# An encoder block with expert retrieval on one core: matmul operands placed at multiples of 512 bytes, two kinds of transfers issued elsewhere and earlier

## The chip, the core and the metric

The kernel runs on one core of a Trainium2 chip. The metric is the device time of one execution, in microseconds; lower is better. The median of three runs of the kernel before is 1516.14 us (1514.39 to 1519.15).

A core has five engines with a queue each: TensorE (PE: matmuls, and PEld, the load of a matmul's stationary operand), VectorE (DVE), ScalarE (ACT), GpSimd (POOL) and SyncE (SP). DMAs are started from the queues of SP, ACT and POOL. Each queue works in order.

## What is computed

512 tokens of 1024 channels go through a mixer (pooling and a short convolution, gated) and then through an expert layer, which holds most of the work:

```python
x = x + m @ w_out[l]                                  # m: the gated mixer
h2 = rmsnorm(x, g_ffn[l])
x = x + peer_ffn(h2, w_q[l], sub_keys[l], expert_u[l], expert_v[l])

# peer_ffn, per token, 8 heads:
q = (hb @ w_q).reshape(PEER_TOKEN_BLOCK, PEER_HEADS, 2, PEER_HALF)
s = jnp.einsum('thpc,hpkc->thpk', q, sub_keys)        # 2 x 128 key scores
top_s, top_i = lax.top_k(s, PEER_TOPK)                # 16 best of each half
cand_s = top_s[:, :, 0, :, None] + top_s[:, :, 1, None, :]
fin_s, fin_pos = lax.top_k(cand_s, PEER_TOPK)         # 16 best pairs -> idx, gates
act = jax.nn.gelu(jnp.einsum('thkd,td->thk', expert_u[idx], hb))
out = jnp.einsum('thk,thkd->td', gates * act, expert_v[idx])
```

There are 16384 experts (128 x 128), and each token uses 8 x 16 of them.

## The kernel before

All matmuls of width 256 to 512 work on a high and a low part of each operand (`split` makes them, `mm3` issues the three products, lines 58 to 60). The order of all work is the order of the code: a manual schedule, with nothing reordered. The stages, with the time at which they run:

- **Mixer** (to about 290 us). Weights come as `raw` tiles through `w_plan`, are split into `wh` and `wl` (ACT copies, POOL or DVE subtracts), and are the stationary operands; the normed input `hH`, `hL` (or the branches' `pHL`, `yHL`) is the moving one, 512 columns wide. In the output projection the mixer's result `mH`, `mL` is stationary and the weights move. A weight tile is laid out as [partition, k, 256], and a matmul takes 128 of the 256.
- **Queries and keys** (290 to 510 us). `load_q` brings and splits the query weights, `queries` multiplies them with `h2H`, `h2L`, VectorE picks the top 16s. Between them `u_tick` already runs chunks of the expert layer.
- **Chunks of the up projection.** There are 128 chunks of 128 experts. For each, `u_load` (SP) brings `ur`, `u_high` and `u_low` split it into `uH`, `uL`, `u_mm` does 24 matmuls of 320 columns with `uH`, `uL` stationary, and `u_act` writes `a` (ACT, a Gelu) and, for the first 76 chunks, stores it to `Ad` in HBM from ACT's queue.
- **Building the gates** (about 510 to 780 us, 48 steps). Dense gates of 384 tokens are built by matmuls of one-hots: `one_hots` (DVE compares, ACT scales by `cgate`), 8 products of 128 x 128 on line 858, `to_stage` (ACT copies the result into `stage`). When a stage of 32 tokens is full, ACT stores it to `Gd` in two halves of 1 MB (line 766); 11 of the 12 stages go there. Each step also holds one chunk of the up projection (`u_load(i + 3)`, `u_high(i + 2)`, `u_low(i + 2)`), and two calls of `gather`: for the last 128 tokens, and for the up projection of 64 of the 384, rows of experts are gathered (POOL) and multiplied on VectorE (lines 719, 724), expert by expert. Near the end the dot products of those 64 tokens, `mdots`, go through a Gelu (ACT, line 835) and a product with `mgate` (DVE, line 836), and then through `mgates` (PE, line 824) into `cgate`.
- **Outputs** (about 780 to 1500 us, 128 steps). Step i loads `expert_v` (`v_load`, split into `vH`, `vL`), the gates of four chunks at a time (`g_load`, 704 KB) and the stored activations (`a_load`), forms `wH`, `wL` = gates x activations (`weigh`, `weigh_low`), and does 18 matmuls of 512 columns (line 904) with `wH`, `wL` stationary and `vH`, `vL` moving. From step 75 on, each step also holds one chunk of the up projection.

Where the tiles lie in a partition follows from the pools' order of allocation. In the built program of the kernel before, the starts of TensorE's operands stand this many bytes past a multiple of 512: `uH`, `uL` 352; `vH`, `vL`, `wH`, `wL` 96; `mH`, `mL` 160; `wh`, `wl` 480; `gwH`, `gwL` 416; `hH`, `h2H` and their low parts 256; `pHL`, `yHL` 416; the one-hots 96. So no stationary tile of 128 columns (512 bytes) starts at a multiple of 512, and each runs over one.

Of the kernel before, what the change touches and what calls it, by code (L numbers as in the profile page):

```python
# [16 lines left out]
P = 128  # L17
D = 1024
T = 512
# [28 lines left out]
def block_kernel(ctx: ExitStack, tc: tile.TileContext, io, out, dbg=None):  # L48
# [3 lines left out]
    def split(Hd, Ld, src, pool=False):  # L52

        nc.scalar.copy(Hd, src)  # L54
        (nc.gpsimd if pool else nc.vector).tensor_tensor(Ld, src, f(Hd), ALU.subtract)  # L55
# [13 lines left out]
    def rbank(lo=0, hi=8):  # L69
        ring[0] += 1  # L70
        return bank(lo + ring[0] % (hi - lo))

    keep = ctx.enter_context(tc.tile_pool(name="keep", bufs=1))
    work = ctx.enter_context(tc.tile_pool(name="work", bufs=2))

# [3 lines left out]

    for tag, w, n in (("u", T, 2), ("s", T, 2), ("p", T, 2), ("up", T + 2, 2), ("sg", T, 4)):  # L80
        fpool.tile([P, w], F32, tag=tag, name=tag, bufs=n)
    pHL = fpool.tile([P, 2, 4, T], F32R, tag="pHL", name="pHL")
    pH, pL = pHL[:, 0], pHL[:, 1]
# [5 lines left out]
    gb = fpool.tile([P, D], F32, tag="gb", name="gb")  # L89
    w0 = [wpool.tile([P, DC, 256], t, tag=n, name=n) for n, t in (("raw", F32), ("wh", F32R), ("wl", F32R))]  # L90

# [3 lines left out]
    def w0_load(e):  # L95
        nc.sync.dma_start(w0[0][:, :, e * P:(e + 1) * P], io["w_in"][0, :, :, e * P:(e + 1) * P])

# [11 lines left out]

    warm = keep.tile([P, 1], F32, name="warm")  # L110
    nc.vector.memset(warm, 1.0)
    nc.scalar.activation(warm, warm, AF.Sqrt)
    cold = fpool.tile([P, T], F32, tag="sg", name="cold", bufs=4)
    nc.vector.memset(cold, 0.0)
    for k in range(4):
        nc.tensor.matmul(bank(7), cold[:, :P], cold, start=True, stop=True)
    pscale = keep.tile([P, 4], F32, name="pscale")
    nc.gpsimd.dma_start(pscale, io["pool_scale"])
    cw = keep.tile([P, 12], F32, name="cw")
    nc.gpsimd.dma_start(cw, io["conv_w"])  # L120
# [3 lines left out]
    nc.gpsimd.iota(iota, pattern=[[1, P]], base=0, channel_multiplier=0, allow_small_or_imprecise_dtypes=True)  # L124
    rcnt = fpool.tile([P, 4, 16], F32, name="rcnt")
    for g, w in enumerate((2, 4, 8, 16)):
# [43 lines left out]
    raws_w, ws_q = {}, []  # L170

    def w_load(k):

        if k < len(w_plan):
            src, n, m, _, _ = w_plan[k]
            raws_w[k] = wpool.tile([P, n, m], F32, tag="raw", name="raw")
            nc.sync.dma_start(raws_w[k], src)
# [3 lines left out]
    def w_next():  # L181

        k = n_w[0]
        n_w[0] += 1
        if k < len(w_plan):
            _, n, m, pool, dst = w_plan[k]
            wh, wl = dst() if dst else [wpool.tile([P, n, m], F32R, tag=t, name=t) for t in ("wh", "wl")]
            split(wh, wl, raws_w.pop(k), pool=pool)
            w_load(k + 2)
            ws_q.append((wh, wl))  # L190
# [4 lines left out]
    def z_part(o, w, u, t0, t1):  # L195
        for k in range(DC):
            mm3(o[:, t0:t1], w[0][:, k, u * P:(u + 1) * P], w[1][:, k, u * P:(u + 1) * P], hH[:, k, t0:t1], hL[:, k, t0:t1],
                k == 0, k == DC - 1)

# [30 lines left out]
    def w0_split(e):  # L230
        es = slice(e * P, (e + 1) * P)
        nc.scalar.copy(w0[1][:, :, es], w0[0][:, :, es])
        for k in (slice(0, 4), slice(4, 8)):
            nc.gpsimd.tensor_tensor(w0[2][:, k, es], w0[0][:, k, es], f(w0[1][:, k, es]), ALU.subtract)

# [104 lines left out]
    def branch(w, aH, aL, u):  # L340
        o = rbank()
        for k in range(4):
            mm3(o, w[0][:, k, u * P:(u + 1) * P], w[1][:, k, u * P:(u + 1) * P], aH[:, k], aL[:, k], k == 0, k == 3)
        return o
# [26 lines left out]

    nc.scalar.activation(warm, warm, AF.Sqrt)
    hn = keep.tile([P, NT - KD, D], F32, name="hn")
# [93 lines left out]
    def load_q(h):  # L467
        raw = wpool.tile([P, DC, 256], F32, tag="raw", name="raw")
        wh = wpool.tile([P, DC, 256], F32R, tag="wh", name="wh")
        wl = wpool.tile([P, DC, 256], F32R, tag="wl", name="wl")  # L470
        nc.sync.dma_start(raw, io["w_q"][h])
        nc.scalar.copy(wh, raw)
        for k in (slice(0, 4), slice(4, 8)):
            nc.gpsimd.tensor_tensor(wl[:, k], raw[:, k], f(wh[:, k]), ALU.subtract)
        return wh, wl
# [20 lines left out]

    rank0 = qpool.tile([P, TOPK], F32, name="rank0")
    nc.vector.tensor_scalar(rank0, iota[:, :TOPK], 2.0, 1.0, op0=ALU.mult, op1=ALU.max)
# [27 lines left out]
    def queries(w, s):  # L526
        o = bank(2 + s)
        for k in range(DC):
            mm3(o, w[0][:, k, s * P:(s + 1) * P], w[1][:, k, s * P:(s + 1) * P], h2H[:, k], h2L[:, k], k == 0, k == DC - 1)
        q = qpool.tile([P, T], F32, tag="q", name="q", bufs=2)  # L530
        nc.scalar.copy(q, o)
        return q
# [93 lines left out]
    gate = qpool.tile([P, NT, H, TOPK], F32, tag="sc2", name="gate", bufs=1)  # L626
    zs = qpool.tile([P, NT, H], F32, tag="zs", name="zs", bufs=1)
    nc.vector.tensor_tensor(gate, fv, fv[:, :, :, 0:1].to_broadcast([P, NT, H, TOPK]), ALU.subtract)
# [124 lines left out]

    built, stages = {}, {}

    def to_stage(n):

        t1 = 4 * n % TG
        if t1 == 0:
            stages[0] = (lpool if (4 * n // TG) % 2 == (NG - 1) % 2 else spool).tile([P, NK, TG], F32, tag="stage", name="stage")  # L760
        stage = stages[0]
        nc.scalar.copy(stage[:, :, t1:t1 + 4], built.pop(n).rearrange("p (t i) -> p i t", t=4))
        if t1 + 4 == TG and 4 * n // TG < NG - 1:
            for q in range(2):
                ks = slice(q * 64, q * 64 + 64)
                nc.scalar.dma_start(Gd[4 * n // TG, :, ks], stage[:, ks])

# [16 lines left out]
    def a_load(i):  # L784
        if i < n_ahead:
            abs_[i] = bpool.tile([P, TU], F32, tag="ab", name="ab", bufs=3)
            nc.sync.dma_start(abs_[i], Ad[i])
# [41 lines left out]
    for n in range(0, TD // 4, 2):  # L829
        left = TD // 4 - n  # L830
        if TM and left == TM // 4 + 6:

            assert n_done[0] >= NM
            ms_ = mdots[:, TM:2 * TM]
            nc.scalar.activation(ms_, ms_, AF.Gelu)
            nc.vector.tensor_tensor(ms_, ms_, mgate, ALU.mult)
        i = nu[0]
        nu[0] += 1
        u_load(i + 3)
        u_high(i + 2)  # L840
        one_hots(n + 2)
        if n:
            to_stage(n - 2)
            to_stage(n - 1)
# [3 lines left out]
        if left == 4:  # L848
            g_load(0)
            a_load(0)  # L850
            a_load(1)
        if 24 <= left < 30:
# [104 lines left out]
    for i in range(NK - 1):  # L957
        v_load(i + 3)
        g_load(i + 2)
        g_rest(i + 2)  # L960
        a_load(i + 2)
        both = i + 1 >= n_ahead
# [26 lines left out]

    nc.scalar.activation(warm, warm, AF.Sqrt)  # L990
    last = range(NK - 3, NK)
# [71 lines left out]
```

## Time and profile before

| | |
|---|---|
| median of three runs | 1516.14 us |
| the profiled execution, its own time | 1516.17 us |
| its span, first to last instruction | 1514.4 us |
| PE busy | 1469.5 us, 97% |
| DVE busy | 1209.5 us, 80% |
| ACT, POOL busy | 682.2 us, 694.5 us |
| moved by DMA | 415.7 MB, 275 GB/s over the span |

The profile has one line per group of instructions, stretches of the span with the busy time of each engine, what each wait was for, and the start of each instruction. Matmuls are pipelined, so a busy PE says little: what one matmul costs is read from the distance between the starts of matmuls that follow each other without a wait. A wait counts if the engine that waits is the one that sets the pace of its stage.

### The profile page before, as it was taken

What the parts mean: (1) busy time and instruction counts of PE and PEld (TensorE: products, weight loads), DVE (VectorE), ACT (ScalarE), POOL (GpSimd) and SP (SyncE); (2) the same over time, 40 slices, a digit from 0 to 9 for tenths busy, and PEclk for the clock granted to TensorE, in tenths of its full rate; (3) what the DMA queues carried; (4) which work ended last, traced back from release to release, by engine and by line L of the source; (5) the groups of instructions that cost most, each with busy time, mean ns of one, the idle gap of its engine ahead of it and who ended that gap; (6) DMA issues with size and microseconds to landing.
All of it is one profiled execution on the core that took longest, in us unless ns stands there. A gap on an engine that the chain in (4) does not pass through costs nothing.

```text
span 1514.4 us, 22020 instructions
## 1 busy us (share of the span) xinstructions
PE 1469.5 (97%) x7953; PEld 1289.3 (85%) x7953; DVE 1209.5 (80%) x2238; ACT 682.2 (45%) x1196; POOL 694.5 (46%) x432
## 2 busy tenths in 40 slices
PE   8999999999997989999999999999999999999997
PEld 6788888878887989999897878888889999999996
DVE  5841433549999899999877888888899999999975
ACT  4323223433324678878763433333333343333434
POOL 3432322337774577766223333333255555556610
PEclk9999999999999999999999999999999999999999
DMA  5222223442213799999989999999999999999951
GB/s 188 84 98 84 84 97 113 128 162 111 111 55 126 277 373 385 401 386 395 361 309 373 351 363 372 359 350 374 363 380 388 378 387 387 390 383 380 394 210 70
DMA packets 163356, 415.71 MB, mean 275 GB/s; under 512 B 13744, under 2 KB 80304, under 8 KB 156848
## 3 DMA queue, kind: packets, MB, share of 16 engines
q1 hardware_dynamic: 102992, 210.99, 39.0%
q0 software_dynamic: 46144, 167.80, 28.9%
q10 hardware_dynamic: 14112, 35.53, 6.1%
q8 instruction: 62, 1.02, 0.3%
q14 instruction: 46, 0.38, 0.1%
HBM read 376.05 MB, written 37.62 MB: 273 GB/s over the span
## 4 chain that ended last, share of the span: by engine, by line
PE 69%; DVE 17%; DMA 8%; ACT 4%; issue 2%; ACTq 1%; POOL 0%; DVEq 0%; SPq 0%; POOLq 0%
PE b L904 31%; PE b L59 12%; PE b L58 12%; PE b L60 12%; DMA Ad<-a 5%; DVE hot L800 2%; DMA ab<-Ad 2%; PE b L858 2%; DVE uL L434 1%; ACT hot L815 1%; DVE gr L719 1%; DVE eq L583 1%; DVE key L597 1%; DVE sc L517 1%; DVE ti L515 1%
## 5 line engine op out<-in xcount | busy, mean ns | idle before, releaser
L58 PE MATMUL b<-h2H,uH 128*128 128x320 f32 x1024 | 322.6, 315 | 10.7 <-ACT a L451 8.6
L60 PE MATMUL b<-h2H,uL 128*128 128x320 f32 x1024 | 317.2, 310 | 7.9 <-DVE uL L434 7.9
L59 PE MATMUL b<-h2L,uH 128*128 128x320 f32 x1024 | 317.1, 310 | 1.0 <-DVE h2L L55 1.0
L707 POOL DMA_INDIRECT gr<-in_expert_u,gidx x128 | 174.0, 1359 | 251.4 <-DVE dots L719 157.4
L707 POOL DMA_INDIRECT gr<-in_expert_v,gidx x128 | 164.6, 1286 | 193.2 <-DVE x L724 106.8
L904 PE MATMUL b<-vH,wH 128*128 128x512 f32 x768 | 238.7, 391 | 3.3 <-ACT wH L888 3.3
L904 PE MATMUL b<-vH,wL 128*128 128x512 f32 x768 | 238.6, 391 | 0.0
L904 PE MATMUL b<-vL,wH 128*128 128x512 f32 x768 | 237.4, 390 | 0.0
L873 ACT CAST vH<-vr 128x1024 fp32r<-128x1024 f32 x128 | 134.8, 1053 | 173.1 <-PE b L904 120.3
L58 PEld LDWEIGHTS b<-h2H,uH 128*128 128x128 f32 x1024 | 193.3, 189 | 16.1 <-ACT a L451 11.9
L877 DVE TENSOR_TENSOR vL<-vr,vH 128x1024 fp32r<-128x1024 f32 x128 | 156.6, 1224 | 61.6 <-ACT vH L873 61.2
L60 PEld LDWEIGHTS b<-h2H,uL 128*128 128x128 f32 x1024 | 193.1, 189 | 9.0 <-DVE uL L434 9.0
L59 PEld LDWEIGHTS b<-h2L,uH 128*128 128x128 f32 x1024 | 193.3, 189 | 3.2 <-DVE h2L L55 1.2
L904 PEld LDWEIGHTS b<-vH,wL 128*128 128x128 f32 x768 | 142.8, 188 | 33.5 <-DVE wL L895 4.2
L904 PEld LDWEIGHTS b<-vL,wH 128*128 128x128 f32 x768 | 144.2, 188 | 30.9
L904 PEld LDWEIGHTS b<-vH,wH 128*128 128x128 f32 x768 | 141.4, 188 | 31.8 <-ACT wH L888 6.2
L724 DVE SCALAR_TENSOR_TENSOR x<-gr,dots,x 128x1024 f32<-128x1024 f32 x128 | 163.8, 1280 | 1.1
L707 POOL DMA_INDIRECT gr<-in_expert_u,midx x64 | 139.5, 2180 | 48.0 <-DVE mdots L719 37.3
L719 DVE CUSTOM_DVE_ANT_0 gr<-gr,hn 128x1024 f32<-128x1024 f32 x128 | 154.3, 1218 | 3.8 <-DMA gr<-in_expert_u,gidx 3.8
L55 POOL TENSOR_TENSOR wl<-raw,wh 128x2048 fp32r<-128x2048 f32 (+1 forms) x21 | 79.3, 3775 | 155.9 <-ACT wh L54 155.9
L434 DVE TENSOR_TENSOR uL<-ur,uH 128x1024 fp32r<-128x1024 f32 x113 | 139.9, 1239 | 11.7 <-ACT uH L430 11.6
L430 ACT CAST uH<-ur 128x1024 fp32r<-128x1024 f32 x128 | 134.0, 1048 | 27.7 <-ACT a L451 23.6
(217 smaller groups left out, 2452.9 us busy)
## 6 DMA issues: line engine op xcount, KB each, us to landing
ur<-in_expert_ut SPq DMA_DIRECT2D x128, 512.0 KB, 7.8
vr<-in_expert_v SPq DMA_DIRECT2D x128, 512.0 KB, 6.7
Gd<-stage ACTq DMA_DIRECT2D x22, 1024.0 KB, 10.1
gt<-Gd SPq DMA_DIRECT2D x32, 704.0 KB, 9.5
raw<-in_w_in SPq DMA_DIRECT2D x15, 1024.0 KB, 4.9
Ad<-a ACTq DMA_DIRECT2D x76, 160.0 KB, 6.3
ab<-Ad SPq DMA_DIRECT2D x76, 160.0 KB, 8.5
raw<-in_w_q SPq DMA_DIRECT2D x8, 1024.0 KB, 6.4
```

The lines of the kernel that those rows point to most:

```text
L55: (nc.gpsimd if pool else nc.vector).tensor_tensor(Ld, src, f(Hd), ALU.subtract)
L58: nc.tensor.matmul(o, lh, rh, start=first, stop=False)
L59: nc.tensor.matmul(o, lh, rl, start=False, stop=False)
L60: nc.tensor.matmul(o, ll, rh, start=False, stop=last)
L430: nc.scalar.copy(us[i][0], raws[i])
L434: eng.tensor_tensor(us[i][1], raws.pop(i), f(us[i][0]), ALU.subtract)
L707: nc.gpsimd.indirect_dma_start(out=r, out_offset=None, in_=io["expert_u" if kind == "u" else "expert_v"], in_offset=bass.IndirectOffsetOnA ...
L719: nc.vector.tensor_tensor_reduce(out=r, in0=r, in1=src, op0=ALU.mult, op1=ALU.add, scale=1.0, scalar=0.0, accum_out=dst)
L724: nc.vector.scalar_tensor_tensor(x1[:, KD + g], r, dots[:, g, k:k + 1], x1[:, KD + g], op0=ALU.mult, op1=ALU.add)
L873: nc.scalar.copy(vs[i][0], vraw[i])
L877: nc.vector.tensor_tensor(vs[i][1], vraw.pop(i), f(vs[i][0]), ALU.subtract)
L904: nc.tensor.matmul(acc[tb][hf], lw[:, ts], rw[:, hf * 512:(hf + 1) * 512], start=i == 0 and rw is vH and lw is wH, stop=last and i == NK - 1)
```

## The change

Three things are changed.

**Placement.** The pools and small tiles are allocated in another order and padded so that in the built program every operand of TensorE starts at a multiple of 512 bytes (the identity's second half, used once, stands at 256). The weight tiles `wh`, `wl` of 256 columns are laid out as [partition, 2, k, 128] in place of [partition, k, 256], so that the 128 columns of successive k lie 512 bytes apart. The copies and subtractions that make them therefore read and write in runs of 128 elements.

**Gates.** A full stage is put on a list, and `stage_out` stores it at the start of the next step, from SP's queue, ahead of that step's `u_load`. The product of `mdots` with `mgate` stands behind the step's one-hots.

**Outputs.** `ab` has 4 buffers in place of 3; three of its tiles are loaded ahead in place of two; in the loop `a_load(i + 3)` comes before `g_load(i + 3)`, where `g_load(i + 2)` came before `a_load(i + 2)`.

```diff
+    work = ctx.enter_context(tc.tile_pool(name="work", bufs=2))
+    for _ in range(3):
+        work.tile([P, 5, 1], F32, tag="rms", name="st", bufs=3)
     keep = ctx.enter_context(tc.tile_pool(name="keep", bufs=1))
-    work = ctx.enter_context(tc.tile_pool(name="work", bufs=2))
+    edge = ctx.enter_context(tc.tile_pool(name="edge", bufs=1, side="right"))
+    warm = edge.tile([P, 120], F32, name="warm")
+    pscale = keep.tile([P, 4], F32, name="pscale")
+    cw = keep.tile([P, 12], F32, name="cw")
+    rank0 = keep.tile([P, 48], F32, name="rank0")[:, :TOPK]
...
+    rcnt = fpool.tile([P, 7, 16], F32, name="rcnt")[:, :4]
...
             _, n, m, pool, dst = w_plan[k]
-            wh, wl = dst() if dst else [wpool.tile([P, n, m], F32R, tag=t, name=t) for t in ("wh", "wl")]
-            split(wh, wl, raws_w.pop(k), pool=pool)
+            raw = raws_w.pop(k)
+            if m == 2 * P:
+
+                wh, wl = [wpool.tile([P, 2, n, P], F32R, tag=t, name=t) for t in ("wh", "wl")]
+                split(by_k(wh), by_k(wl), raw.rearrange("p k (u m) -> p k u m", u=2), pool=pool)
+            else:
+                wh, wl = dst() if dst else [wpool.tile([P, n, m], F32R, tag=t, name=t) for t in ("wh", "wl")]
+                split(wh, wl, raw, pool=pool)
...
-            mm3(o[:, t0:t1], w[0][:, k, u * P:(u + 1) * P], w[1][:, k, u * P:(u + 1) * P], hH[:, k, t0:t1], hL[:, k, t0:t1],
-                k == 0, k == DC - 1)
+            mm3(o[:, t0:t1], w[0][:, u, k], w[1][:, u, k], hH[:, k, t0:t1], hL[:, k, t0:t1], k == 0, k == DC - 1)
...
         if t1 + 4 == TG and 4 * n // TG < NG - 1:
+            full.append((4 * n // TG, stage))
+
+    def stage_out():
+
+        while full:
+            s, stage = full.pop()
             for q in range(2):
                 ks = slice(q * 64, q * 64 + 64)
-                nc.scalar.dma_start(Gd[4 * n // TG, :, ks], stage[:, ks])
+                nc.sync.dma_start(Gd[s, :, ks], stage[:, ks])
...
             nc.scalar.activation(ms_, ms_, AF.Gelu)
-            nc.vector.tensor_tensor(ms_, ms_, mgate, ALU.mult)
         i = nu[0]
         nu[0] += 1
+        stage_out()
         u_load(i + 3)
         u_high(i + 2)
         one_hots(n + 2)
+        if TM and left == TM // 4 + 6:
+            nc.vector.tensor_tensor(ms_, ms_, mgate, ALU.mult)
...
         v_load(i + 3)
-        g_load(i + 2)
-        g_rest(i + 2)
-        a_load(i + 2)
+        a_load(i + 3)
+        g_load(i + 3)
+        g_rest(i + 3)
```

What moves on the queues. First SP's queue, at the end of the stage that builds the gates and the start of the outputs (`Gd` and `Ad` are the gates and activations in HBM, `gt` and `ab` their tiles on the way back). Before:

```order
L425 DMA ur<-in_expert_ut 128x1024 x10
L774 DMA gt<-Gd 128x11x128
L787 DMA ab<-Ad 128x320 x2
L425 DMA ur<-in_expert_ut 128x1024 x5
L953 DMA gfin<-in_g_final 128x1024
L752 DMA vr<-in_expert_v 128x1024
L787 DMA ab<-Ad 128x320
```

And now:

```order
L785 DMA Gd<-stage 128x2048 x2
L438 DMA ur<-in_expert_ut 128x1024 x2
L793 DMA gt<-Gd 128x11x128
L806 DMA ab<-Ad 128x320 x3
L438 DMA ur<-in_expert_ut 128x1024 x5
L974 DMA gfin<-in_g_final 128x1024
L765 DMA vr<-in_expert_v 128x1024
L806 DMA ab<-Ad 128x320
```

The stores of `stage` stand in SP's queue now, two per stage and four `ur` loads apart in all of the build; the last pair stands two `ur` loads ahead of the first `gt`.

ACT's queue at the end of the step in which a stage becomes full, from the cast of a chunk's high part on. Before:

```order
L815 ACTIVATE hot<-hot,cgate 128x128 x8
L762 COPY stage<-b_4773 128x128x4
L762 COPY stage<-b_4778 128x128x4
L766 DMA Gd<-stage 128x2048 x2
L451 ACTIVATE a<-b_4806 128x320
L453 DMA Ad<-a 128x320
```

And now:

```order
L834 ACTIVATE hot<-hot,cgate 128x128 x8
L775 COPY stage<-b_4779 128x128x4
L775 COPY stage<-b_4784 128x128x4
L464 ACTIVATE a<-b_4810 128x320
L466 DMA Ad<-a 128x320
```

The two stores between the copies and the next `a` are gone from ACT.

DVE's queue around the product of `mdots` with `mgate`. Before:

```order
L719 ISA mdots 128x1
L434 TENSOR_TENSOR uL<-ur,uH 128x1024
L836 TENSOR_TENSOR mdots<-mdots,mgate 128x64
L800 TENSOR_TENSOR hot<-iota,ckey 128x2x512
L809 TENSOR_TENSOR hot<-iota,ckey 128x512
L812 TENSOR_SCALAR hot<-iota,ckey,cgate 128x128 x4
```

And now:

```order
L732 ISA mdots 128x1
L447 TENSOR_TENSOR uL<-ur,uH 128x1024
L819 TENSOR_TENSOR hot<-iota,ckey 128x2x512
L828 TENSOR_TENSOR hot<-iota,ckey 128x512
L831 TENSOR_SCALAR hot<-iota,ckey,cgate 128x128 x4
L862 TENSOR_TENSOR mdots<-mdots,mgate 128x64
```

The product moved behind six instructions of the same step. TensorE's queue holds the same matmuls in the same order.

## Rows read from the trace of the kernel before

**Rows 1.** Stretches: us, busy us of each engine (x instructions), PEclk, DMA share, GB/s.
```profile
50.00:280.00 230.00, 230.00 (x990) 185.50 (x990) 92.60 (x93) 64.87 (x69) 74.72 (x20) 1.00 0.29 101
...
340.00:480.00 140.00, 133.75 (x754) 119.38 (x753) 138.37 (x781) 48.31 (x75) 103.28 (x65) 0.99 0.28 101
...
590.00:750.00 160.00, 151.40 (x1122) 149.32 (x1121) 153.27 (x186) 129.97 (x324) 97.97 (x47) 1.00 1.00 391
...
950.00:1100.00 150.00, 149.76 (x656) 121.92 (x655) 126.69 (x175) 58.36 (x83) 49.15 (x44) 1.00 1.00 362
...
1200.00:1300.00 100.00, 100.00 (x553) 90.63 (x553) 92.74 (x122) 39.31 (x57) 56.67 (x43) 1.00 1.01 386
```

**Rows 2.** Timeline of PE, mixer: start us, us, engine line op out<-in xcount.
```profile
99.98 0.39 PE L58 MATMUL b<-hH,wh 128*128 128x512 f32 x1
...
101.85 0.39 PE L60 MATMUL b<-hH,wl 128*128 128x512 f32 x1
```

**Rows 3.** Timeline of PE, one step of the outputs, matmuls of lines 904 and 58.
```profile
1201.92 0.62 PE L904 MATMUL b<-vH,wH 128*128 128x512 f32 x2
...
1204.19 0.62 PE L904 MATMUL b<-vH,wL 128*128 128x512 f32 x2
1204.64 0.31 PE L58 MATMUL b<-h2H,uH 128*128 128x320 f32 x1
...
1208.02 0.31 PE L60 MATMUL b<-h2H,uL 128*128 128x320 f32 x1
```

**Rows 4.** Groups by line: xcount | busy us, mean ns of one | idle before.
```profile
L904 PE MATMUL b<-vH,wH 128*128 128x512 f32 x768 | 238.7, 391 | 3.3 <-ACT wH L888 3.3
...
L58 PE MATMUL b<-hH,wh 128*128 128x512 f32 (+1 forms) x272 | 104.4, 384 | 0.2 <-ACT hH L54 0.2
...
L58 PE MATMUL b<-h2H,wh 128*128 128x512 f32 x128 | 51.5, 403 | 0.0
```

**Rows 5.** Waits of 505 to 750 us: engine line <- released by: us, times, longest.
```profile
DVE uL L434 <- ACT uH L430: 4.2, 4, 1.8
DVE gr L719 <- DMA gr<-in_expert_u,gidx: 3.8, 1, 3.8
DVE mdots L836 <- ACT mdots L835: 2.9, 1, 2.9
DVE hot L800 <- PE b L858: 1.4, 3, 1.1
...
PE b L58 <- ACT a L451: 8.6, 10, 1.9
...
ACT a L451 <- DMA Ad<-a: 7.5, 5, 2.3
...
ACT a L451 <- issue: 4.6, 2, 2.3
```

**Rows 6.** Timeline of ACT where a stage is stored, and the chain's longest piece.
```profile
560.90 2.20 ACTq L766 DMA_DIRECT2D Gd<-stage  x2
563.20 0.44 ACT L451 ACTIVATE a<-b 128x320 f32<-128x320 f32 x1 [2.33 <-issue]
...
539.34 16.27 DMA Ad<-a
```

**Rows 7.** Timeline: a step of DVE, and one chunk's load and use.
```profile
579.65 1.05 ACT L430 CAST uH<-ur 128x1024 fp32r<-128x1024 f32 x1 [0.40 <-ACT a L451]
...
582.38 1.22 DVE L434 TENSOR_TENSOR uL<-ur,uH 128x1024 fp32r<-128x1024 f32 x1
...
583.63 0.33 SPq L425 DMA_DIRECT2D ur<-in_expert_ut  x1
584.04 0.81 ACTq L766 DMA_DIRECT2D Gd<-stage  x2
...
585.83 1.05 ACT L430 CAST uH<-ur 128x1024 fp32r<-128x1024 f32 x1 [0.44 <-ACT a L451]
...
588.01 1.22 DVE L434 TENSOR_TENSOR uL<-ur,uH 128x1024 fp32r<-128x1024 f32 x1
...
596.00 1.06 ACT L430 CAST uH<-ur 128x1024 fp32r<-128x1024 f32 x1 [0.40 <-ACT a L451]
```

**Rows 8.** DMA issues: xcount, KB each, median us from issue to landing.
```profile
ur<-in_expert_ut SPq DMA_DIRECT2D x128, 512.0 KB, 7.8
...
Gd<-stage ACTq DMA_DIRECT2D x22, 1024.0 KB, 10.1
```

**Rows 9.** Outputs' start: SP's issue, and waits of 790 to 1100 us.
```profile
798.38 6.50 SPq L787 DMA_DIRECT2D ab<-Ad  x1
...
DVE gt L885 <- DMA ab<-Ad: 3.4, 3, 1.7
PE b L904 <- ACT wH L888: 3.3, 5, 1.6
```

## What the time will be: the prediction

> **What bounds the kernel now.** I read the stretches first [rows 1], then the distance between starts of matmuls [rows 2, 3], then the waits of each stretch [rows 5, 9]. The stretches tell which engine sets the pace where. From 50 to 280 us PE is busy for 230 of 230 us and DVE for 93: PE alone. From 340 to 480 us DVE is busy for 138.4 of 140 us: VectorE's top 16s set the pace, and PE's matmuls are cheap there. From 590 to 750 us, while the gates are built, DVE has 153.3 of 160 us; two of its casts of one kind are 5.63 us apart with no gap between [rows 7]. From 950 to 1100 us and from 1200 to 1300 us PE has no gap again, DVE 84% and 93%, and the DMA engines are busy throughout, at 362 and 386 GB/s; the most that a long stretch shows is 391 GB/s.
>
> So in over 900 of the 1514 us the time is the number of matmuls times the distance between them. The granted clock there is 1.00, its upper level of 2.4 GHz, at which 512 columns stream in 213.3 ns and 320 in 133.3 ns. The rows show more. In the mixer, with `wh` stationary, 8 starts take 101.85 - 99.98 = 1.87 us, 233.8 ns each, 20.4 over the stream [rows 2]. In the outputs 10 starts take 1204.19 - 1201.92 = 2.27 us, 227.0 ns, 13.7 over; 23 starts of the 320-wide ones take 3.38 us, 147.0 ns, 13.7 over [rows 3].
>
> **The change part by part.** The profiled execution took 1516.17 us (span 1514.4 us), which is the median; every sum starts from 1516.
>
> *Placement.* No row of before shows a stationary tile that starts at a multiple of 512 bytes, so its price has to be bounded. One end is that nothing moves: the starts 96 (`wH`) and 352 (`uH`) past a multiple of 512, with moving operands at 96 and 256, all cost the same 13.7 ns over the stream [rows 3]. Where a tile begins within 512 bytes does not matter between these. The other end is that all that lies over the stream comes from running over such a boundary, since every one of them does. A third value lies between: only `wh`, at 480 past with just 32 bytes ahead of the boundary and 1024 bytes from k to k, is slower, by 233.8 - 227.0 = 6.8 ns. The new placement takes away both of these peculiarities, and `wh` would go to the pace of the others. I take this value, as it is the only dependence on place that rows show. It holds for 3 x 272 matmuls of the mixer, less the 96 narrow ones, so 720 [rows 4], and, counted in the code, for some 192 of the branches: 912 x 6.8 ns = 6.2 us, in a stretch that PE bounds. The 3 x 128 of the queries [rows 4] would give 2.6 us, but DVE sets the pace there: nothing. Against this stand the copies into the new layout, in runs of 128; POOL is busy for 75 of 230 us there [rows 1], so a subtraction somewhat slower is hidden. I take 5 us gained, with the ends 0 and, under the second rival, 80.
>
> The Trainium skill's page "TensorE: Matmul & The Clock Gate", section "Back-to-back issue gap", gives N / 2.4 + 2.5 ns and has no term for an operand's place; by it 320 columns would be 135.8 ns apart, where the rows show 147.0. The trace disagrees with it in every stage, and the page does not say whether the placement is the reason.
>
> *Gates from SP's queue.* Where a stage is stored, ACT is held by the two issues: 2.20 us in the worst case, and the next `a` comes 2.33 us late [rows 6]. Behind it the store of `a` lands late; the chain has a piece of 16.27 us for it [rows 6], and in all ACT waits 7.5 us for that and 4.6 us for issue [rows 5]. PE waits 8.6 us for `a` [rows 5]. But PE does not set the pace here, so its 8.6 us are not what comes back. DVE's own waits are: 4.2 us for `uH` from a late ACT [rows 5], which goes with the issue gone. The 3.8 us for a gather and 1.4 us for PE stay. Gained: 4 us, between 0 and the 8.6 of PE.
>
> What the move adds: the stores now stand in SP's queue ahead of a `ur` load. That load is issued at 583.63 us, and its cast runs at 596.00 us: 12.4 us, of which landing takes 7.8 [rows 7, 8], so 4.6 us are to spare. The stores wait for ACT's copies, which end just before their issue at 584.04 us [rows 7], so the load goes out about 0.4 us plus two issues of 0.4 us later: 1.2 us. It then queues behind two stores of 1 MB each [rows 8], which at 391 GB/s pass in 5.4 us: 6.6 us in all, 2.0 more than there is to spare. Then ACT stands still at the cast, with the one-hots behind it. DVE feels it as far as its subtraction comes too early: it starts 1.7 and 1.1 us after the cast's end (582.38 - 580.70, 588.01 - 586.88) [rows 7], some 1.4 us of slack. So a late load costs at least 2.0 - 1.4 = 0.6 us in each of 11 stages, 7 us; and nothing, if 16 engines take up the load before the stores are through. I take the middle, 3.5 us, which cancels the gain of 4 but for half a microsecond: I carry this part as zero, between -8.6 and the third rival's +58.
>
> The skill's page "DMA: Bandwidth & Descriptors", section "Issuing engines are not separate DMA queues", says that transfers from all queues run on the same 16 engines, and that another issuer only saves issue time. By it only the share of the 4.6 us for issue comes back and the late `a` stores (7.5 us) stay, and the sum would be 2 us higher. The row on the 16.27 us speaks for more: a store of 160 KB stuck behind 2 MB.
>
> *The product with mgate behind the one-hots.* DVE waits 2.9 us for ACT's Gelu [rows 5]; now it compares the one-hots meanwhile. DVE sets the pace: 3 us gained, 0 if the next step's wait for `cgate` takes it.
>
> *Activations and gates for the outputs.* SP is held for 6.50 us at an `ab` load that stands behind a `gt` load [rows 9]; in the new order `ab` goes first. DVE's 3.4 us for `ab` and PE's 3.3 us for `wH` are the same stall [rows 9], in a stretch that PE bounds. 2.5 us gained, between 0 and 3.3.
>
> **The sum:** 1516 - 5 - 0 - 3 - 2.5 = 1505.5, so **1505 us**. Without any of the placement 1510; with all the bounds of the moves (8.6 + 2.9 + 3.3) 1496.
>
> **Rivals.**
>
> *All of the 13.7 ns goes with the placement.* For it: the amount is the same for widths 320 and 512, as a fixed cost of each stationary tile would be, and all tiles run over a boundary. Against it: it does not depend on how much of the tile lies ahead of the boundary. The price: 912 x 20 + 192 (output projection) x 14 = 21 us in the mixer; the outputs' 3 x 768 [rows 4] x 13.7 = 31.6 us, and 53 chunks x 24 x 13.7 = 17.4 us beside them; together 70, and 5.5 of the moves: 1440. But transfers cap it: from 950 to 1100 us 391 over 362 GB/s leaves 8%, more than the 6% asked for (18.5 us over 75 steps); from 1100 on, with 385 GB/s, only 1.6% of 385 us, 6 us in place of 30. With the cap 21 + 18.5 + 6 + 5.5 = 51: 1465. Between the two, **1455 us** (1440 to 1480), as gathers can shift a little.
>
> *The page's pace.* By the page's 2.5 ns over the stream the same rival would end some 15 us higher without the cap; it lies within that range, and gets no chance of its own.
>
> *The placement does nothing, and the moves little.* For it: equal cost at three placements [rows 3]; the DMA engines' share is 1.00 while the gates are built, at the highest rate of the trace [rows 1], so a wait that goes may come back as a later landing. Half of the 5.5 us: **1513 us** (1508 to 1518).
>
> *Slower: the loads of `ur` behind the stores.* The point from which it decides is the 4.6 us and DVE's 1.4. If the two stores need not 5.4 us but the 10.1 us that their landing takes now [rows 8], since gathers share the engines, the load is late by 1.2 + 10.1 - 4.6 = 6.7 us, and DVE by 5.3; over 11 stages 58 us. The middle between 0.6 and 5.3 is 3 us, over 11 stages 32, less the 10.5 of the other parts: **1537 us** (1521 to 1564). The skill's page on DMA, section "Queues, rings and completion order", has descriptors of one ring consumed in order, which is how a load behind a store would wait; no row of before shows a load behind a store on one queue.
>
> **How the numbers follow.** The forecast of 1505 has a chance of 0.35 (1496 to 1511): it asks only for what rows show as a difference. The first rival has 0.28: its price is large but rests on no row with another placement. That little changes has 0.20; slower has 0.17, since by the full rate alone the load is late already. What a measurement of this kernel can tell from no change is about 0.3%, 4.5 us, so faster is below 1511.6 and slower above 1520.7. Faster: 0.35 + 0.28 + 0.06 of the third = 0.69. Within 0.3%: the other 0.14 and 0.02 of the last: 0.16. Slower: 0.15. The range has to reach into the first rival; from 1440 to 1524 it leaves out about 0.04 below and 0.13 above.
>
> **What would show it.** Placement: starts of matmuls in the mixer at 227 ns (forecast), 234 (nothing) or near 214 to 216 (first rival, with 320-wide ones at 133 to 136); if DMA caps it, PE's waits for `vH`, `wH` or `uH` grow in the outputs, with 390 GB/s or more. Gates: no wait of ACT for issue and none of DVE for `uH` between 505 and 750 us; if the loads are late, ACT's cast of `uH` waits for the DMA of `ur`, which it hardly does now. Outputs: no 6.5 us on SP at `ab`. I would be wrong if a matmul got slower at the new places, or if the stage of queries, where DVE sets the pace, changed.

## The result and the profile after

The changed kernel takes **1557.38 us** (median; 1555.67 to 1560.54); the kernel before, run beside it, 1515.66. The ratio is **1.0276, 95% interval 1.0256 to 1.0296**: 42 us slower. The forecast was 1505 us with a range of 1440 to 1524, and the time lies outside it. It lies inside that of the third rival (1521 to 1564), whose place is the right one and whose mechanism, as the runs show, is not.

Where the 39.5 us between the two spans (1514.4 and 1553.9 us) came in is read from the first and last starts of TensorE's lines. The view is that of one line's instructions: duration in ns (min/median/max), first and last start in us. Before (line 58 is the up projection's first product, 858 the gates, 904 the outputs):

```profile
L58 PE MATMUL b<-h2H,uH x1024: 307/310/468, 295.9 to 1493.2; 128*128 128x320 f32 x171
...
L858 PE MATMUL b<-hot x768: 272/275/276, 508.7 to 777.8; 128*128 128x128 f32 x192
...
L904 PE MATMUL b<-vH,wH x768: 387/389/504, 792.0 to 1505.2; 128*128 128x512 f32 x192
```

And after (lines 58, 879, 925):

```profile
L58 PE MATMUL b<-h2H,uH x1024: 302/309/636, 290.1 to 1532.7; 128*128 128x320 f32 x171
...
L879 PE MATMUL b<-hot x768: 270/275/583, 503.6 to 813.6; 128*128 128x128 f32 x192
...
L925 PE MATMUL b<-vH,wH x768: 389/389/628, 830.9 to 1544.7; 128*128 128x512 f32 x192
```

| stretch | before, us | after, us | difference |
|---|---|---|---|
| start to the first chunk (the mixer) | 295.9 | 290.1 | -5.8 |
| first chunk to the first gate matmul | 212.8 | 213.5 | +0.7 |
| building the gates, first to last gate matmul | 269.1 | 310.0 | **+40.9** |
| last gate matmul to the first output | 14.2 | 17.3 | +3.1 |
| outputs, first to last | 713.2 | 713.8 | +0.6 |

The stretches of the changed kernel that answer to [rows 1] (us, busy us of PE, PEld, DVE, ACT, POOL with instructions, PEclk, DMA share, GB/s):

```profile
50.00:280.00 230.00, 229.86 (x1019) 190.06 (x1018) 96.22 (x101) 67.01 (x73) 74.97 (x20) 1.00 0.29 101
...
590.00:750.00 160.00, 138.11 (x950) 135.57 (x949) 131.20 (x146) 111.97 (x287) 87.72 (x44) 0.94 0.90 334
...
950.00:1100.00 150.00, 150.00 (x661) 123.31 (x660) 127.52 (x184) 58.96 (x83) 51.26 (x44) 1.00 1.00 366
```

Two things stand out. From 50 to 280 us PE, busy throughout as before, gets through 1019 matmuls where it did 990. From 590 to 750 us no engine sets the pace any more: DVE, 153.3 of 160 us before, is busy for 131.2, PE for 138.1, and the DMA engines' share is 0.90. Something else is waited for. The granted clock of 0.94 there goes with PE's own waits: from 598 to 606 us, where PE is busy for 6.35 of 8 us, it is 0.79. From 590 to 638 us it is 0.93, and 1.00 with the stores back on ACT (the first run below). What the clock adds to the waits by itself was not measured.

The waits of 505 to 830 us name it (engine, line, released by: us, times, longest; the last two rows are SP's queue):

```profile
ACT uH L443 <- DMA ur<-in_expert_ut: 80.4, 13, 9.7
DVE uL L447 <- ACT uH L443: 56.8, 15, 7.0
...
PE b L879 <- ACT hot L834: 28.1, 8, 4.7
...
SPq L785 <- ACT a L464: 104.1, 9, 12.2
...
SPq L785 <- ACT stage L775: 22.9, 2, 12.0
```

Against [rows 5], ACT now stands 80.4 us for the loads of `ur`, and DVE, which sets the pace of the build, 56.8 us behind it, 49.5 of them in the build (up to 814 us), in place of 4.2. The build lost 40.9. PE stands 28.1 us behind both. The last two rows are the ones to look at: SP, whose own time nobody counts, stands 104.1 + 22.9 = 127.0 us at line 785, the new store, 11.5 us at each of the 11 stages. One stage in the timeline:

```profile
585.84 1.05 ACT L775 COPY stage<-b 128x512 f32<-128x512 f32 x2
...
586.91 0.81 SPq L785 DMA_DIRECT2D Gd<-stage  x2
...
587.63 1.05 ACT L443 CAST uH<-ur 128x1024 fp32r<-128x1024 f32 x1 [0.41 <-ACT a L464]
587.83 4.09 SPq L438 DMA_DIRECT2D ur<-in_expert_ut  x3
...
598.25 1.04 ACT L443 CAST uH<-ur 128x1024 fp32r<-128x1024 f32 x1 [5.94 <-DMA ur<-in_expert_ut]
```

The stores go out when ACT's copy has ended, at 586.91 us. Behind them three loads of `ur` go out in a burst, where before one went out every 5.63 us. The chain of waits has the first of them, from its issue to its landing:

```profile
587.83 10.40 DMA ur<-in_expert_ut
```

587.83 + 10.40 = 598.23 us, and there the cast starts, after ACT has waited 5.94 us. In all the chain of waits holds ten such pieces of 10.3 to 13.1 us between 533 and 787 us.

### The profile page after: what moved, and what is told of

Same layout as the page of the kernel before. It is cut to its first block, busy times and chain, and to the rows that moved or that the text cites. A ratio compares the mean times of both kernels' runs of the same rounds, so it can differ in the third digit from the quotient of the medians.

```text
span 1553.9 us, 21982 instructions
## 1 busy us (share of the span) xinstructions
PE 1477.5 (95%) x7953; PEld 1305.5 (84%) x7953; DVE 1209.5 (78%) x2238; ACT 680.1 (44%) x1196; POOL 686.2 (44%) x432
## 4 chain that ended last, share of the span: by engine, by line
PE 64%; DVE 19%; DMA 10%; issue 3%; ACT 2%; SPq 1%; POOL 0%; ACTq 0%; DVEq 0%; POOLq 0%
PE b L925 33%; PE b L60 10%; PE b L59 10%; PE b L58 10%; DMA ur<-in_expert_ut 8%; DVE hot L819 3%; DVE gr L732 2%; DVE uL L447 2%; DVE key L610 1%; DVE eq L596 1%; DVE sc L530 1%; DVE ti L528 1%; DVE ti L534 1%; DMA vr<-in_expert_v 1%; DVE tv L526 1%
## 5 line engine op out<-in xcount | busy, mean ns | idle before, releaser
L443 ACT CAST uH<-ur 128x1024 fp32r<-128x1024 f32 x128 | 134.1, 1048 | 99.2 <-DMA ur<-in_expert_ut 80.4
L720 POOL DMA_INDIRECT gr<-in_expert_u,midx x64 | 131.6, 2057 | 85.6 <-DVE mdots L732 74.9
```

The lines of the kernel that those rows point to most:

```text
L443: nc.scalar.copy(us[i][0], raws[i])
L720: nc.gpsimd.indirect_dma_start(out=r, out_offset=None, in_=io["expert_u" if kind == "u" else "expert_v"], in_offset=bass.IndirectOffsetOnA ...
```

## The experiments

Three theories stood after the result. **A1**: SP is held at the store, and the loads behind it go out late. **A2**: a load is late because 2 MB stand ahead of it in its queue. **C**: the gates are innocent, and the placement or the outputs cost the time.

### The stores back on ACT

```diff
         if t1 + 4 == TG and 4 * n // TG < NG - 1:
-            full.append((4 * n // TG, stage))
+            for q in range(2):
+                ks = slice(q * 64, q * 64 + 64)
+                nc.scalar.dma_start(Gd[4 * n // TG, :, ks], stage[:, ks])
...
-        stage_out()
         u_load(i + 3)
```

> The changed kernel with the stages stored from ACT's queue again, as before; placement, product and outputs stay changed. Theory A (the loss lies in the stores on SP alone): the build takes 269 us as before, not 310, the mixer keeps its 5.8 us, and the time is 1504 to 1508 us, faster than before by about 0.6%. Rival C (the placement, or the order of the outputs, slows the build or the outputs): the time stays above 1530 us and ACT still waits for the loads of ur.

Measured: 1507.71 us, ratio to before 0.9961 (0.9948 to 0.9975). The gate matmuls take 267.3 us, and ACT waits 5.5 us for `ur` from 505 to 830 us:

```profile
L880 PE MATMUL b<-hot x768: 270/275/421, 502.6 to 769.9; 128*128 128x128 f32 x192
...
ACT uH L443 <- DMA ur<-in_expert_ut: 5.5, 4, 4.5
```

The whole loss is gone; C falls.

### The stores on SP alone

The diff is against the kernel before; `stage_out` is that of the change.

```diff
+            full.append((4 * n // TG, stage))
...
+        stage_out()
         u_load(i + 3)
```

> The kernel before with only the stores of the stages moved to SP's queue, a step later. Theory A: the whole loss appears, and more than in the changed kernel, since nothing is gained beside it: 1557 + 10 = 1567 us (1558 to 1572), with ACT waiting some 80 us for the loads of ur. Rival C: within 5 us of 1516.

Measured: 1562.37 us, ratio 1.0325 (1.0310 to 1.0340). ACT waits 78.9 us for `ur`, DVE 55.2 us for `uH`, and the build takes 311.4 us:

```profile
L865 PE MATMUL b<-hot x768: 272/275/582, 508.6 to 820.0; 128*128 128x128 f32 x192
...
ACT uH L430 <- DMA ur<-in_expert_ut: 78.9, 12, 8.4
```

One edit makes all of the loss.

### The placement alone

The diff is the first part of the change, with the stores, the product and the outputs' loads as before.

> The kernel before with the new placement alone. Theory A: the mixer ends 5.8 us earlier (matmuls with wh stationary 227 ns apart in place of 234), the queries gain nothing since DVE sets the pace there, the outputs nothing, as the 227 and 147 ns there stay: 1510 us (1509 to 1512). Rival C: slower than 1516.

Measured: **1503.98 us, ratio 0.9937 (0.9924 to 0.9949)**: the fastest kernel of the study, ahead of both. The first chunk starts at 290.2 us in place of 295.9, so 5.7 us are the mixer's. The gain was larger than I had expected, 9.5 us with an interval of 7.7 to 11.5: 2 to 6 us of it are not the mixer's. In the profiled execution the build is 4.7 us shorter, too (264.4 us for 269.1, from 503.0 to 767.4). Whether the placement does that is open, since the build varied between 264 and 272 us among the kernels here that store from ACT.

### The stores two and three steps later in SP's queue

The diff is that of two steps; with three the 2 is a 3.

```diff
-            full.append((4 * n // TG, stage))
+            full.append((nu[0] + 2, 4 * n // TG, stage))
...
-    def stage_out():
+    def stage_out(end):

-        while full:
-            s, stage = full.pop()
+        while full and (end or full[0][0] <= nu[0]):
+            _, s, stage = full.pop(0)
...
-        stage_out()
+        stage_out(left == 4)
```

> The changed kernel, but a stage is stored from SP two steps after it is full in the order of SP's queue, not one (the last one as soon as the first gates are loaded back). SP's queue runs some two steps ahead of the other engines, so the store is reached when the stage is just full. Theory A1 (SP is held at the store for about 12 us, and three loads of ur behind it go out late): the hold is nearly gone and with it nearly all of the loss, 1500 to 1512 us. Theory A2 (a load of ur is late because 2 MB stand ahead of it in its queue, as the third rival of the prediction had it): the loads stay late by 2 to 7 us at each of 11 stages, and the time stays above 1525 us.

> The changed kernel, a stage stored from SP three steps after it is full in the order of SP's queue (the last one as soon as the first gates are loaded back). Now the stage is full a step before SP reaches the store, so no hold is left; with two steps SP was still held 66 us in all. Theory A1 alone (the hold is all): ACT's wait for ur falls from 32 us to under 8, the build from 269 to 264 us, and the time to 1501 to 1506 us. Theory A2 (2 MB ahead of a load also cost): ACT's wait for ur stays above 20 us and the time at 1508 to 1513 us.

Measured: 1510.55 us with two steps, ratio 0.9970 (0.9958 to 0.9982), and 1507.96 us with three, ratio 0.9947 (0.9927 to 0.9966). One or two steps' difference in where two instructions stand in a queue is worth 47 to 49 us. With two steps SP is still held, for half as long as in the changed kernel: 61.2 + 5.2 = 66.4 us, 6.0 at each stage. The waits of 505 to 830 us with two steps:

```profile
ACT uH L443 <- DMA ur<-in_expert_ut: 32.5, 15, 4.7
...
SPq L785 <- ACT a L464: 61.2, 10, 7.1
...
SPq L785 <- ACT stage L775: 5.2, 1, 5.2
```

So half of the hold costs little, if anything. In the kernel before, the load that goes out at 578.00 us is cast at 590.92, 12.9 us later, of which landing takes 7.8 [rows 8]: by these, as an estimate, some 5 us of a hold are free. The waits of 505 to 830 us with three steps:

```profile
ACT uH L443 <- DMA ur<-in_expert_ut: 21.3, 11, 3.6
...
DVE uL L447 <- ACT uH L443: 11.4, 5, 6.8
...
SPq L785 <- ACT a L464: 7.2, 5, 2.0
...
SPq L785 <- ACT stage L775: 4.4, 1, 4.4
```

SP waits for ACT at the store for 11.6 us in all in place of 127.0. What A2 claims is there as well, but small: ACT still waits 21.3 us for loads, where with the stores on ACT it was 5.5. So with almost no hold a load behind 2 MB does land late, by about 2 us a stage (21.3 / 11). DVE hardly feels it: 6.8 of its 11.4 us come after the build, and the 4.6 us in it stand against 5.5 with the stores on ACT. In the whole time it does not show, either: the intervals of the stores on SP (0.9927 to 0.9966) and on ACT (0.9948 to 0.9975) overlap. A1 is the loss. I had expected 1501 to 1506 for the hold alone; whether A2 has a part in the 2 us above that is not shown.

### The hold without the bytes

The first part is in `to_stage`, as in the kernel before; the second in `stage_out`.

```diff
+    Hd = dram.tile([TD // TG - 1, P, 1], F32, name="Hd")
...
+            for q in range(2):
+                ks = slice(q * 64, q * 64 + 64)
+                nc.scalar.dma_start(Gd[4 * n // TG, :, ks], stage[:, ks])
             full.append((4 * n // TG, stage))
...
-                nc.sync.dma_start(Gd[s, :, ks], stage[:, ks])
+            nc.sync.dma_start(Hd[s], stage[:, NK - 1, TG - 1:TG])
```

> The changed kernel, but the 2 MB of a stage are stored from ACT as before, and what stands on SP in their place, at the same point, is a store of one column of the stage (512 bytes in all) to a place that nobody reads. The wait stays on SP, the bytes are gone from it. Theory A1 (the hold is the loss): the build takes 300 us or more and the time is 1540 us or more, ACT waits over 60 us for ur. Theory A2 (the bytes ahead are the loss): the build takes 270 us and the time is under 1515 us. Both in part: between.

Measured: 1603.77 us, ratio 1.0590 (1.0568 to 1.0613). With 512 bytes in place of 2 MB on SP the loss is not smaller, it doubles. The waits (505 to 860 us) and one stage's load in the chain:

```profile
ACT uH L444 <- DMA ur<-in_expert_ut: 107.6, 11, 13.8
...
SPq L787 <- ACT stage L776: 119.0, 11, 12.9
```

```profile
591.18 14.88 DMA ur<-in_expert_ut
```

SP is held as in the changed kernel, 119.0 us over 11 stages. The load that is let go then takes 14.9 us here (14.4 to 17.9 over the stages) against 10.4 above (10.3 to 13.1): it goes out at the same moment as ACT's 2 MB. DVE waits 95.1 us behind ACT, and the build takes 357.8 us (501.6 to 859.4) in place of 310.0. So a late load beside another queue's 2 MB fared worse here than one behind 2 MB of its own queue. That the hold makes a loss without the bytes on SP's queue is shown; how large it is without those 2 MB beside it is not. What the hold would cost with no store anywhere wasn't tried, since the gates are read back.

### The two small moves

The stages are stored from ACT in both. The first part of the diff alone (the product ahead of the one-hots again), then the second alone (the outputs' loads as before):

```diff
             nc.scalar.activation(ms_, ms_, AF.Gelu)
+            nc.vector.tensor_tensor(ms_, ms_, mgate, ALU.mult)
...
-        a_load(i + 3)
-        g_load(i + 3)
-        g_rest(i + 3)
+        g_load(i + 2)
+        g_rest(i + 2)
+        a_load(i + 2)
```

> The new placement and the new order of the outputs' loads; the product of mdots with mgate stands ahead of the one-hots again, and the stages are stored from ACT. Placement alone measured 1504.0 us, placement with product and outputs 1507.7: one of the two small moves costs time, against the prediction, which had 3 and 2.5 us gained. Theory O (the earlier load of 704 KB of gates and the third ab stand ahead of other loads at the start of the outputs): 1506 to 1509 us here. Theory M (the product behind the one-hots): 1502 to 1505 us here. Prediction: 1501.5.

> The new placement and the product of mdots with mgate behind the one-hots; the order of the outputs' loads as before, stages stored from ACT. Theory O: 1502 to 1505 us. Theory M: 1506 to 1509 us. Prediction: 1501, the wait of 2.9 us for the Gelu gone from DVE.

Measured: placement and outputs 1509.86 us, ratio 0.9971 (0.9958 to 0.9984); placement and product 1508.25 us, ratio 0.9948 (0.9930 to 0.9967). By their times, for which the two expectations were written, the two runs speak for different theories: 1509.86 us stands just above the range of theory O, and 1508.25 in that of theory M. They ran beside other executions of the kernel before than the placement alone did, so I compare ratios. The product: 0.9948 against 0.9937 for the placement alone, 0.9961 against 0.9971 for placement and outputs: up once and down once by 0.1%, nothing that can be told. The outputs: 0.9971 against 0.9937 and 0.9961 against 0.9948, up both times, the first beyond the intervals: about 0.1 to 0.3%, 2 to 5 us **lost** by the medians, of which only the first difference is clear. The waits of 765 to 830 us show where. With the stores on ACT and the outputs changed:

```profile
ACT vH L895 <- DMA vr<-in_expert_v: 6.2, 2, 3.9
...
PE b L926 <- ACT wH L910: 3.8, 2, 2.7
```

And with the placement alone:

```profile
ACT vH L894 <- DMA vr<-in_expert_v: 3.4, 3, 1.6
...
DVE gt L906 <- DMA ab<-Ad: 1.6, 1, 1.6
PE b L925 <- ACT wH L909: 1.5, 3, 1.1
```

The wait for `ab` is gone, as meant, and a longer one for `vr` has come. The other two runs agree: with the outputs changed PE waits 3.7 us for `wH`, with the old order 1.7. So the traces show some 2 us of loss. SP's timeline at the first `gt` of the loop has the reason, first the changed order, then, in the second fence, the old one:

```profile
783.50 0.52 SPq L795 DMA_DIRECT2D gt<-Gd  x1
789.03 5.46 SPq L765 DMA_DIRECT2D vr<-in_expert_v  x1
```

```profile
786.91 0.44 SPq L795 DMA_DIRECT2D gt<-Gd  x1
787.62 6.53 SPq L808 DMA_DIRECT2D ab<-Ad  x1
```

SP is held behind the 704 KB of `gt` in both: before for 6.50 us at `ab` [rows 9], now for 5.46 us at the `vr` that stands there. `vr` feeds ACT's cast of `vH`, and ACT's next `wH` is queued behind that cast; the load that was let through first was the less urgent one.

### What about the placement is worth 6.8 ns

The first edit brings back the old layout. The second moves `wh`, `wl` and `raw` from 0 to 256 past a multiple of 512; without the tile (`warm` lies in the padding of `rank0` then) they start at 480. The stages are stored from ACT in all four.

```diff
-wh, wl = [wpool.tile([P, 2, n, P], F32R, tag=t, name=t) for t in ("wh", "wl")]
+wh, wl = [wpool.tile([P, n, 2, P], F32R, tag=t, name=t).rearrange("p k u m -> p u k m") for t in ("wh", "wl")]
...
-    warm = edge.tile([P, 120], F32, name="warm")
+    warm = edge.tile([P, 56], F32, name="warm")
```

> The new placement with the stages stored from ACT, but wh and wl laid out as [partition, k, 256] again, starting at a multiple of 512 bytes. It tells which of wh's two peculiarities cost the 6.8 ns. Theory S (the start: only 32 of a tile's 512 bytes ahead of a boundary): 227 ns from start to start in the mixer, as every tile of 128 columns still starts at a multiple of 512. Theory K (the 1024 bytes from k to k): 234 ns.

> The new placement and layout [partition, 2, k, 128], with the stages stored from ACT, but wh, wl and raw start 480 bytes past a multiple of 512, as before; all moving operands stay at multiples of 512. Theory S: 234 ns in the mixer. Theory K: 227 ns. A third (M: the moving operand's place, 256 past before, made the 6.8 ns together with wh's): 227 ns here, too, and at e9_k256.

> As the run at 480, with wh, wl and raw 256 bytes past a multiple of 512. Theory S: 227 ns, as uH at 352 and wH at 96 cost no more than at a multiple of 512. Theory K or M: 227 ns. A price that grows with the part of the tile behind the boundary would be between 227 and 234.

> As the run at 480, with the old layout [partition, k, 256] as well: wh stands as in the kernel before in both respects, and only the other operands are at multiples of 512. Theory S or K: 234 ns in the mixer. Theory M (the moving operand's place): 227 ns.

Two starts of line 58 in the mixer, nine matmuls apart, in the timeline of PE. Start at a multiple of 512, layout [k, 256]; 2.04 us, 226.7 ns each:

```profile
98.77 0.39 PE L58 MATMUL b<-hH,wh 128*128 128x512 f32 x1
...
100.81 0.39 PE L58 MATMUL b<-hH,wh 128*128 128x512 f32 x1
```

Start at 480, layout [2, k, 128]; 2.10 us, 233.3 ns each:

```profile
99.11 0.39 PE L58 MATMUL b<-hH,wh 128*128 128x512 f32 x1
...
101.21 0.40 PE L58 MATMUL b<-hH,wh 128*128 128x512 f32 x1
```

| layout | start past a multiple of 512 | ns from start to start | one execution, us |
|---|---|---|---|
| [2, k, 128] (the changed kernel's) | 0 | 226.7 | 1555.67 (stores on SP) |
| [k, 256] | 0 | 226.7 | 1505.63 |
| [2, k, 128] | 256 | 226.7 | 1505.56 |
| [2, k, 128] | 480 | 233.3 | 1511.51 |
| [k, 256] | 480 | 233.3 | 1514.05 |

Of start and layout the start decides (theory S): at 480 a tile pays 6.6 ns whichever the layout, at 0 and 256 it doesn't. It need not be the stationary one. In the output projection `wh` is the moving operand and `mH`, at a multiple of 512, the stationary one; with `wh` at 480 (layout [2, k, 128]) nine matmuls take 2.10 us there, too, 233.3 ns each, and with `wh` at 256 or 0 226.7:

```profile
248.90 0.40 PE L58 MATMUL b<-wh,mH 128*128 128x512 f32 x1
...
251.00 0.40 PE L58 MATMUL b<-wh,mH 128*128 128x512 f32 x1
```

In the kernel before, with `mH` at 160, the same matmuls were 229.1 ns apart in the mean, so the places of both operands count, in a way that these runs do not settle.

The last two rows have every other operand at a multiple of 512, and yet take 1511.51 and 1514.05 us, against 1511.53 for the kernel before beside them. By these single executions all other moves of the placement, `uH` from 352 and `wH` from 96 to 0 among them, and the new layout with its copies, are worth nothing that shows. Against that stand the 2 to 6 us that the placement alone gained beyond the mixer; which of the two holds stays open.

## Why the prediction was wrong, point by point

**What bounds the kernel.** Right. The mixer took its gain one to one, and the build its loss through DVE.

**Placement, 5 us.** Right in its mechanism, and well sized for the mixer: 5.8 us there, nothing in the queries, matmuls at 226.7 ns. The placement alone gained 9.5 us (7.7 to 11.5), and what lies beyond the mixer has no place in the prediction. The value between the two ends was the one that held, for the reason given: the one place with a row of its own. PE's timeline after, two starts nine matmuls apart, against [rows 2]:

```profile
98.63 0.39 PE L58 MATMUL b<-hH,wh 128*128 128x512 f32 x1
...
100.67 0.39 PE L58 MATMUL b<-hH,wh 128*128 128x512 f32 x1
```

The first rival falls: in the outputs, where all tiles start at multiples of 512 now, nothing moved against [rows 3]. Ten starts take 2.27 us and 18 narrow ones 2.64 us, 227.0 and 146.7 ns each (PE's timeline after, one step):

```profile
1241.44 0.61 PE L925 MATMUL b<-vH,wH 128*128 128x512 f32 x2
...
1243.71 0.62 PE L925 MATMUL b<-vH,wL 128*128 128x512 f32 x2
...
1244.16 0.30 PE L58 MATMUL b<-h2H,uH 128*128 128x320 f32 x1
...
1246.80 0.31 PE L58 MATMUL b<-h2H,uH 128*128 128x320 f32 x1
```

So the 13.7 ns over the stream don't come from running over a boundary. What they are stays open. The Trainium skill's figure of 2.5 ns over the stream, which "TensorE: Matmul & The Clock Gate", section "Back-to-back issue gap", gives for a single isolated matmul, isn't reached in this stream of matmuls with operands placed so, either: 227.0 - 213.3 = 13.7. Two figures of the prediction beside its sum are off: the 80 us named as an end of the placement are 70 by the working of the rival that they belong to, the first, and 2.5 ns for each of the 4680 matmuls which that rival counts are 12 us, not 15. The forecast rests on neither.

**Gates from SP, carried as zero.** This is the step that failed, and it failed in one sentence: "the load goes out about 0.4 us plus two issues of 0.4 us later". It took the load that is issued at the time of the stores, 583.63 us, for the one that stands behind them in the queue. The rows ahead of the prediction held the contradiction. A load waits for the buffer that DVE's subtraction frees, and there are three. The load of 583.63 us is cast at 596.00 [rows 7], three steps after the step in which ACT stores, and in the order of the code a load stands one step ahead of its cast: so at the moment of the store SP is already at a load two steps on. SP's queue runs two steps ahead of the other engines. A store that stands one step later in the code is therefore reached by SP some two steps before its stage is full; two steps of 5.63 us [rows 7] are 11.3, and SP was held for 11.5. The load that stands behind the store is the one of 578.00 us, and its cast starts at 590.92. Two views of the timeline before:

```profile
578.00 5.96 SPq L425 DMA_DIRECT2D ur<-in_expert_ut  x2
```

```profile
590.92 1.05 ACT L430 CAST uH<-ur 128x1024 fp32r<-128x1024 f32 x1 [0.40 <-ACT a L451]
```

With that load the prediction's own sum would have given, as an estimate in hindsight: out at 583.63 + 1.2 = 584.8 us, landing 7.8 us later [rows 8], at 592.6; 1.7 us late with nothing ahead of it, and 7.1 with the 5.4 us of the 2 MB. Less DVE's 1.4, that is 0.3 to 5.7 us at each of 11 stages, 3 to 63 us lost. The middle is 33; the build lost 40.9.

**The third rival** had the place (ACT at the cast, DVE behind it, 11 stages) and by its bounds the time: DVE waits 56.8 us for `uH`, and 58 was its upper end. But its mechanism, bytes ahead in the queue, cost ACT about 2 us a load once the hold was gone. The number agreed by accident. The point from which it was to decide, "the 4.6 us", was the slack of the wrong load.

**The product, 3 us.** DVE's wait of 2.9 us for the Gelu is gone from the trace, and no time with it that can be told. Where the stores are on ACT, DVE waits 5.2 us for PE at the one-hots in place of 3.2: the next wait has taken part of its place, and the term's lower end, 0, is what was measured.

**Outputs, 2.5 us.** Wrong in sign, by 2 us of PE's waits in the traces and 2 to 5 us by the medians. The step that failed in this part is "in the new order `ab` goes first": it counted the load that is let through and not the one that takes its place behind `gt`.

## What to carry to other kernels

Before a wait is put into a queue that issues loads, find out how far that queue runs ahead: which buffer each load waits for, and for which step it loads. An instruction that waits for the present must stand about as many steps later there as the queue is ahead, or it stops the prefetch; one or two steps made the difference of 47 to 49 us here. A hold of 6.0 us a stage, near the 5 us or so that the loads had to spare, cost little. And when a load is moved ahead of another, the price is that of the load which now stands behind.

## What the runs showed of the hardware

- A stationary tile of 128 columns (512 bytes a partition) whose start lies 480 bytes past a multiple of 512 put the starts of matmuls 6.6 ns further apart (233.3 against 226.7 ns at 512 columns); starts at 0 and 256 didn't, and those at 96 and 352 hadn't before. With the moving operand at 480 and the stationary one at 0 it was 233.3 ns, too.
- SP issued nothing behind a store that waited for ACT's copies: 127.0 us over 11 stages in the changed kernel, with the loads going out in a burst behind each.
- A load of 512 KB that went out with 2 MB of another queue took 14.4 to 17.9 us (the hold without the bytes), one that went out behind 2 MB of its own queue 10.3 to 13.1 us (the changed kernel); the median over the kernel before is 7.8 [rows 8].
